# Side work spread anew, priority for the score links, and GELU read from PSUM, in a hybrid transformer block

## The chip, the cores and the metric

The kernel runs on one core of a Trainium2 chip. The metric is the device time of one execution in microseconds (us). Engines are named as the profile names them: PE is the matrix engine, DVE the vector engine, ACT the scalar engine, POOL the general-purpose engine, SP the engine that issues the transfers. Each engine works through its own instructions in their written order; semaphores tie the engines together.

## The reference

One block over 512 tokens of width 2048: adaptive RMS norm, a combined projection, a recurrent group beside a forgetting-attention group, an output projection, and a gated MLP.

```python
mod = c_act @ w_ada[l] + b_ada[l]
sh1, sc1, gt1, sh2, sc2, gt2 = jnp.split(mod, 6, axis=-1)
h = modulate(rms_norm(x, g_mix[l]), sh1, sc1)
proj = h @ w_in[l]
xr, yr, q, k, v, f_logit = jnp.split(proj, splits, axis=-1)
y_rec = rglru_group(xr, yr, ...)          # conv, gates, scan; h * gelu(yr)
y_att = forgetting_attention_group(q, k, v, f_logit, ...)
    # s = q k^T + cum_i - cum_j, causal, softmax, times v; cum = cumsum(log_sigmoid(f))
mix = concat([rms_norm(y_rec, g_out_rec), rms_norm(y_att, g_out_att)])
x = x + gt1 * (mix @ w_out[l])
h2 = modulate(rms_norm(x, g_ffn[l]), sh2, sc2)
gate, up = split(h2 @ w_up[l], 2)
x = x + gt2 * ((silu(gate) * up) @ w_down[l])
```

There are 8 heads of width 128, 8 recurrent blocks of 128 channels, and 5632 hidden channels in the MLP.

## The kernel before

Every product of fp32 operands is made of three fp32r matmuls: both operands are split into a high and a low part (ACT writes the high part, L199 or L192; DVE subtracts it, L200 or L193), and PE adds hi·hi, hi·lo and lo·hi in PSUM (L204). The big products run as stages one after the other, each with its own weights streamed in pages of four contraction tiles (k-tiles):

- w1 (recurrent input), yr0 and yr1 (the gate branch), h0 to h7 (q, k, v of one head each: 16 k-tiles of 12 matmuls, 128 tokens by 384 columns), wo0 to wo3 (output projection), up0, up1 and uf4 to uf43 (MLP in), dn (MLP out).

Small work is hung between the k-tiles of a stage as hooks. In stage h(i+1) the hooks carry the attention of head i. `attention` makes the list: statistics of q and k (`stats`: squares on ACT, reduction L480 on DVE, reciprocal root on POOL L253, product L483 on DVE); transposes to PSUM `qkt` (L490) and their copy out on ACT; four `score` blocks; four `pt_` blocks (transpose of the probabilities, L524) and `pv`. A score block is a short chain over three engines: PE writes s (L510), DVE subtracts it from bt with a running minimum (L514, shown as CUSTOM_DVE_ANT_0 in the trace and ISA in the order), ACT takes the exponential (L516), DVE the reciprocal and the scaling (L517, L518). The decay bt comes from cum: the log-forget values lf are made on DVE in some 18 short steps (L300 to L308, then L434), summed on PE (pc, L436), transposed, written to DRAM as cum_d and read back broadcast as cb.

Other hooks are side work of DVE, each with a load of its own:

- The bias of the three first projections, `bias_in`: 48 loads of 256 KB (bw) and as many products (L592, L594) into three accumulators ba. They hang on h1 and h2, three in a row at every second k-tile; two buffers hold the loads. `bias_sum` (L600, tile binp, in h3) adds them up on PE.
- The adaptive scales, `ada1`: products L149 over loads of 512 KB; five in each of h3 to h6 and so on (`H_ADA`), with lowered priority (`ADA_LATE`).

The order on each engine is chosen by a list scheduler that goes by the written order of the hooks and the priorities; `tc.high_priority(offset=...)` moves work ahead, and what it assumes of times need not be what the chip shows. So an instruction may stand in front of another that is ready sooner.

PSUM has eight banks: four "acc", three "misc" and one "rg". Stage yr1 writes the acc banks and is followed by wo0, also on acc; from there on stages alternate between acc and the other four (`bank`). Between yr1 and wo0, the GELU of four of the recurrent tiles is made from yr1's banks: ACT squares the bank, DVE copies it to SBUF (L766), and two DVE steps L767 and L769 with a tanh between them use the copy. Then the sum of squares of the recurrent outputs (L292) is formed, added on PE (`ratioa`), turned to a ratio on POOL (L250, L253, L269), spread by PE (`ratiob`) and copied by ACT; DVE scales the recurrent tiles (L786), which are split (mx0h by ACT, mx0l and so on by DVE) as the last eight k-tiles of wo0's activation. The attention's outputs are the first eight.

Of the kernel before, what the change touches and what calls it, by code (L numbers as in the profile page):

```python
# [62 lines left out]
def block_kernel(ctx, tc, xT, crow, adaT, vecs, bfr, w1, wyr, wqkv0, wqkv, wgate, wout, wup0, wups, wdown, outT):  # L63
# [408 lines left out]
    def attention(h, q, k, v):  # L472
        st = {}

        def stats():
# [29 lines left out]
        def score(b):  # L505
# [8 lines left out]
            nc.vector.tensor_tensor_reduce(out=p[:, :n], in0=ps[:, :n], in1=p[:, :n], scale=-1.0, scalar=3.0e38,  # L514
                                           op0=ALU.add, op1=ALU.min, accum_out=nm)
            nc.scalar.activation(p[:, :n], p[:, :n], AF.Exp, scale=-1.0, bias=nm, accum_out=sm)  # L516
            nc.vector.reciprocal(sm, sm)  # L517
            nc.vector.tensor_scalar_mul(p[:, :n], p[:, :n], sm)  # L518
# [58 lines left out]
    def bias_load(n):  # L577
        kt, j = divmod(n, 3)
        if kt < KT:
            sd = (w1[kt][:, :512], w1[kt][:, 512:], wyr[0][kt // 4][:, (kt % 4) * 512:(kt % 4 + 1) * 512])[j]  # L580
            bias_src[n] = ap_.tile([P, S], F32, tag="x", name=f"bw{kt}_{j}", bufs=2)
            nc.sync.dma_start(out=bias_src[n], in_=sd)

    def bias_in(kt):
        if kt == 0:
            ba.extend(page(f"ba{j}", "c") for j in range(3))
            bias_load(0)
            bias_load(1)
        for j in range(3):
            src, s1 = bias_src.pop(3 * kt + j), sh1[kt]  # L590
            if kt == 0:
                nc.vector.tensor_scalar_mul(ba[j], src, s1)  # L592
            else:
                nc.vector.scalar_tensor_tensor(out=ba[j], in0=src, scalar=s1, in1=ba[j], op0=ALU.mult, op1=ALU.add)  # L594
            bias_load(3 * kt + j + 2)
# [521 lines left out]
```

## Time and profile before

| | us |
|---|---|
| median of 3 runs | 2153.72 (2149.09 to 2156.75) |
| the profiled execution | 2151.9 |
| its span, first to last instruction | 2150.2 |
| PE busy in the span | 2097.6 (98%) |
| DVE busy in the span | 1533.2 (71%) |

Stages by their times in the trace: w1 0 to 97, yr0 to 150, h0 to 186, h1 to 231, h2 to 279, h3 to 332, h4 to 381, h5 to 430, h6 to 476, h7 to 523, yr1 to 574.6, wo0 to 629.4, wo1 to wo3 to 760, up0 and up1 to 849, uf to 1666, dn to the end. A matmul group in the timeline is one row with its count; the number in brackets is the idle time of the engine just before it, with what ended it. [...]

### The profile page before, as it was taken

How to read it: one execution, taken by the hardware profiler on the slowest of the kernel's cores; microseconds unless marked ns; L12 is line 12 of the kernel's file. 1: busy time of each engine (PE TensorE's matmuls, PEld its weight loads, DVE VectorE, ACT ScalarE, POOL GpSimd, SP SyncE). 2: the span in 40 equal slices, each digit the busy share in tenths (PEclk: the TensorE clock that was granted, in tenths of full speed). 3: DMA queues.
4: the chain of work that ended last, by engine and by line, in shares of the span. 5: the costliest groups of instructions: out<-in, count | busy, mean ns of one | idle time of the engine just before them, and what ended most of it. 6: DMA issues, size and time to landing. Idle time of an engine off the chain costs nothing.

```text
span 2150.2 us, 32261 instructions
## 1 busy us (share of the span) xinstructions
PE 2097.6 (98%) x12737; PEld 1903.2 (89%) x12737; DVE 1533.2 (71%) x2407; ACT 858.1 (40%) x1200; POOL 31.3 (1%) x37
## 2 busy tenths in 40 slices
PE   8999899999999999999999999999999999999998
PEld 6888788888878887999999999999999888888887
DVE  8998668887886689988888888888887443323332
ACT  4433337675432245444444444444444222221111
POOL 0000000000010000000000000000000000000000
PEclk9999999999999999999999999999999999999999
DMA  9987666666777732443444443444445975653442
GB/s 334 349 294 267 190 234 202 222 233 227 258 239 250 251 135 98 146 130 128 136 130 128 136 130 128 136 130 128 136 130 184 334 282 172 213 195 135 155 152 97
DMA packets 133017, 406.01 MB, mean 189 GB/s; under 512 B 14561, under 2 KB 19841, under 8 KB 123138
## 3 DMA queue, kind: packets, MB, share of 16 engines
q1 hardware_dynamic: 132866, 403.96, 55.4%
q8 instruction: 99, 1.62, 0.3%
q14 instruction: 52, 0.43, 0.1%
HBM read 361.15 MB, written 42.75 MB: 188 GB/s over the span
## 4 chain that ended last, share of the span: by engine, by line
PE 82%; DVE 9%; DMA 5%; issue 1%; ACT 1%; POOL 1%; SPq 0%; DVEq 0%; ACTq 0%
PE dn_0p L204 6%; PE dn_3p L204 6%; PE dn_1p L204 6%; PE dn_2p L204 6%; PE w1p L204 4%; PE wo0p L204 2%; PE yr1p L204 2%; PE up0p L204 2%; PE wo3p L204 2%; PE wo2p L204 2%; PE wo1p L204 2%; PE yr0p L204 2%; DMA ada<-in_adaT 2%; DMA bw<-in_w 1%; PE h0p L204 1%
## 5 line engine op out<-in xcount | busy, mean ns | idle before, releaser
L149 DVE SCALAR_TENSOR_TENSOR ada<-ada,c_b 128x1024 f32<-128x1024 f32 x128 | 154.8, 1221 | 49.3 <-DMA ada<-in_adaT 48.9
L200 DVE TENSOR_TENSOR uq_0tl<-uq_0r,uq_0th 128x1024 fp32r<-128x1024 f32 x40 | 49.0, 1225 | 61.7 <-ACT uq_0th L199 61.7
L199 ACT ACTIVATE uq_0sh<-uq_0r 128x1024 fp32r<-128x1024 f32 x40 | 42.5, 1062 | 90.8 <-PE uf10p L989 2.3
L200 DVE TENSOR_TENSOR uq_0al<-uq_0r,uq_0ah 128x1024 fp32r<-128x1024 f32 x40 | 49.0, 1225 | 39.1 <-ACT uq_0ah L199 39.1
L199 ACT ACTIVATE uq_1sh<-uq_1rb 128x1024 fp32r<-128x1024 f32 x40 | 42.5, 1062 | 70.6 <-PE uf43p L989 2.4
L199 ACT ACTIVATE uq_0th<-uq_0r 128x1024 fp32r<-128x1024 f32 x40 | 42.4, 1060 | 70.6 <-DVE uq_0r L969 1.9
L199 ACT ACTIVATE uq_1th<-uq_1ra 128x1024 fp32r<-128x1024 f32 x40 | 42.4, 1061 | 69.7 <-PE uf37p L989 1.8
L199 ACT ACTIVATE uq_1ah<-uq_1ra 128x1024 fp32r<-128x1024 f32 x40 | 42.5, 1061 | 60.6 <-issue 59.1
L199 ACT ACTIVATE uq_0ah<-uq_0r 128x1024 fp32r<-128x1024 f32 x40 | 42.4, 1060 | 49.4 <-issue 46.8
L200 DVE TENSOR_TENSOR uq_1tl<-uq_1ra,uq_1th 128x1024 fp32r<-128x1024 f32 x40 | 49.0, 1225 | 10.3 <-ACT uq_1th L199 10.2
L204 PE MATMUL w1p<-hph,w1h 128*128 128x512 f32 x128 | 47.5, 399 | 6.2 <-ACT hph L345 6.2
L594 DVE SCALAR_TENSOR_TENSOR ba<-bw,sh,ba 128x512 f32<-128x512 f32 x45 | 33.4, 749 | 26.0 <-DMA bw<-in_w 14.9
L200 DVE TENSOR_TENSOR uq_1sl<-uq_1rb,uq_1sh 128x1024 fp32r<-128x1024 f32 x40 | 49.0, 1225 | 3.7 <-ACT uq_1sh L199 1.5
L200 DVE TENSOR_TENSOR uq_0sl<-uq_0r,uq_0sh 128x1024 fp32r<-128x1024 f32 x40 | 49.0, 1226 | 3.6
L204 PE MATMUL w1p<-hpl,w1h 128*128 128x512 f32 x128 | 50.9, 398 | 0.0
L204 PE MATMUL w1p<-hph,w1l 128*128 128x512 f32 x128 | 50.7, 396 | 0.0
L200 DVE TENSOR_TENSOR uq_1al<-uq_1ra,uq_1ah 128x1024 fp32r<-128x1024 f32 x40 | 48.7, 1216 | 0.1
L200 DVE TENSOR_TENSOR dn_1l<-dn_2r,dn_1h 128x1024 fp32r<-128x1024 f32 x11 | 13.5, 1226 | 38.1 <-ACT dn_1h L199 38.1
L159 DVE SCALAR_TENSOR_TENSOR ada<-ada,c_b 128x1024 f32<-128x1024 f32 x32 | 39.0, 1218 | 2.3 <-DMA ada<-in_adaT 2.3
L200 DVE TENSOR_TENSOR dn_0l<-dn_2r,dn_0h 128x1024 fp32r<-128x1024 f32 x11 | 13.5, 1225 | 37.6 <-ACT dn_0h L199 37.6
L200 DVE TENSOR_TENSOR dn_1l<-dn_0r,dn_1h 128x1024 fp32r<-128x1024 f32 x11 | 13.5, 1226 | 37.5 <-ACT dn_1h L199 37.3
L200 DVE TENSOR_TENSOR dn_0l<-dn_0r,dn_0h 128x1024 fp32r<-128x1024 f32 x11 | 13.5, 1226 | 36.9 <-ACT dn_0h L199 36.9
(13787 smaller groups left out, 8165.8 us busy)
## 6 DMA issues: line engine op xcount, KB each, us to landing
ada<-in_adaT SPq DMA_DIRECT2D x160, 512.0 KB, 5.5
uq_0r<-in_wups SPq DMA_DIRECT2D x80, 512.0 KB, 4.1
uq_1ra<-in_wups SPq DMA_DIRECT2D x40, 512.0 KB, 4.0
uq_1rb<-in_wups SPq DMA_DIRECT2D x40, 512.0 KB, 3.3
adf<-in_adaT SPq DMA_DIRECT2D x32, 512.0 KB, 6.0
actd<-ach SPq DMA_DIRECT2D x44, 256.0 KB, 2.1
actd<-acl SPq DMA_DIRECT2D x44, 256.0 KB, 4.1
dn_0r<-in_wdown SPq DMA_DIRECT2D x11, 1024.0 KB, 5.1
```

What stands on the lines that cost most here:

```text
L149: nc.vector.scalar_tensor_tensor(out=t, in0=t, scalar=1.0, in1=cs, op0=ALU.mult, op1=ALU.mult, accum_out=ac)
L159: nc.vector.scalar_tensor_tensor(out=t, in0=t, scalar=1.0, in1=c_b[:, cs], op0=ALU.mult, op1=ALU.mult, accum_out=ada_acc[j][:, hf, i:i + 1])
L199: nc.scalar.activation(R(hi[:, :n]), raw_ap, AF.Copy)
L200: tail_lo.append(nc.vector.tensor_sub(R(lo[:, :n]), raw_ap, hi[:, :n]).ins)
L204: nc.tensor.matmul(ps, lhsT=R(l), rhs=R(r), start=start, stop=stop)
L594: nc.vector.scalar_tensor_tensor(out=ba[j], in0=src, scalar=s1, in1=ba[j], op0=ALU.mult, op1=ALU.add)
```

## The change

1. `bias_in` handles one product at a time, one at each hook `n * 2 // 3` of h1 and h2, with the loads six ahead in pages of tag "c" rather than two buffers. The lowered priority of the adaptive products is dropped, and their hooks move a little.
2. In attention, the norm (L483) becomes a step of its own, three k-tiles (in the last head one) behind the start. The copy of the transposes out of PSUM, the score's DVE and ACT links, and the copy of the transposed probabilities get the priority offset `EVAC` (2500).
3. The GELU's copy to SBUF is gone: L767 and L769 read the PSUM bank. wo0 writes misc and rg, and all later stages use the other set than before; the sums for the three norm factors use acc banks.

```diff
-H_ADA = (3, 4, 7, 10, 14)
+H_ADA = (1, 4, 7, 10, 13)
-ADA_LATE = -300
+BIAS_AHEAD = 6
...
-        with tc.high_priority(offset=ADA_LATE), tc.issue_after(tail_lo[-1]):
+        with tc.issue_after(tail_lo[-1]):
...
             rms_rstd(ss, ss, HEAD_DIM)
+            st["ss"] = ss
+
+        def norm():
+            ss = st["ss"]
             for a, z in ((0, q), (1, k)):
...
-                nc.scalar.activation(zt, pt, AF.Copy, scale=g)
+                with tc.high_priority(offset=EVAC):
+                    nc.scalar.activation(zt, pt, AF.Copy, scale=g)
...
+            with tc.high_priority(offset=EVAC):
+                nc.vector.tensor_tensor_reduce(out=p[:, :n], in0=ps[:, :n], in1=p[:, :n], scale=-1.0, scalar=3.0e38,
+                                               op0=ALU.add, op1=ALU.min, accum_out=nm)
+                nc.scalar.activation(p[:, :n], p[:, :n], AF.Exp, scale=-1.0, bias=nm, accum_out=sm)
+                nc.vector.reciprocal(sm, sm)
+                nc.vector.tensor_scalar_mul(p[:, :n], p[:, :n], sm)
...
-            nc.scalar.activation(pT[:, qs], pt[:, qs], AF.Copy)
+            with tc.high_priority(offset=EVAC):
+                nc.scalar.activation(pT[:, qs], pt[:, qs], AF.Copy)
...
-            bias_src[n] = ap_.tile([P, S], F32, tag="x", name=f"bw{kt}_{j}", bufs=2)
+            bias_src[n] = page(f"bw{kt}_{j}", "c")
...
+    def bias_in(n):
+        if n == 0:
+            ba.extend(page(f"ba{j}", "c") for j in range(3))
+            for m in range(BIAS_AHEAD):
+                bias_load(m)
+        kt, j = divmod(n, 3)
+        src, s1 = bias_src.pop(n), sh1[kt]
         if kt == 0:
...
+        bias_load(n + BIAS_AHEAD)
...
-    ATT_STEPS = (None, 6, 8, 8, 9, 9, 12, 12, 13, 13, 14, 14, 15, 15)
-    LAST_STEPS = (None, 3, 5, 5, 6, 6, 9, 9, 10, 10, 13, 13, 13, 13)
+    ATT_STEPS = (None, 3, 6, 8, 8, 9, 9, 12, 12, 13, 13, 14, 14, 15, 15)
+    LAST_STEPS = (None, 1, 3, 5, 5, 6, 6, 9, 9, 10, 10, 13, 13, 13, 13)
...
-            for kt in range(8):
-                add(hk, kt * 2, lambda kt=kt + 8 * h: bias_in(kt))
+            for n in range(24):
+                add(hk, n * 2 // 3, lambda n=n + 24 * h: bias_in(n))
...
-        g, w = page(f"gy{f}", "c"), page(f"ge{4 + f}", "c")
+        g, w = yr1[f], page(f"ge{4 + f}", "c")
         nc.scalar.activation(w, yr1[f], AF.Square)
-        nc.vector.tensor_copy(out=g, in_=yr1[f])
...
-    rec_sums, rec_spread = rstd_parts(ssq_rec, D_REC, "ratio", times=att_rms)
+    rec_sums, rec_spread = rstd_parts(ssq_rec, D_REC, "ratio", times=att_rms, bank=acc)
...
-        ps = fm_group(wout[g], korder, mix, f"wo{g}", hooks=hk, ps=[bank(g, f, f"wo{g}p{f}") for f in range(4)])
+        ps = fm_group(wout[g], korder, mix, f"wo{g}", hooks=hk, ps=[bank(g + 1, f, f"wo{g}p{f}") for f in range(4)])
...
-        pb = acc(f"bup_p{gi}") if gi % 2 else misc(f"bup_p{gi}")
+        pb = misc(f"bup_p{gi}") if gi % 2 else acc(f"bup_p{gi}")
...
-        ps = [bank(f, b, f"uf{f}p{b}") for b in range(4)]
+        ps = [bank(f + 1, b, f"uf{f}p{b}") for b in range(4)]
...
-            ps = [bank(g + pi, f, f"dn{pi}_{g}p{f}") for f in range(4)]
+            ps = [bank(g + 1, f, f"dn{pi}_{g}p{f}") for f in range(4)]
```

The order of the instructions moves at many places. Three of them follow; a tile's trailing number only tells copies of a tile apart. DVE in stage h1, before, at the end of the log-forget steps (lf; ba<-bw are bias products, h_1l a weight split):

```order
L307 TENSOR_SCALAR lf<-lf 128x32
L616 TENSOR_TENSOR xrl_2739<-xrl_2739,rstd_x 128x512
L200 TENSOR_TENSOR h_1l<-h1r_1999,h_1h 128x768
L306 TENSOR_TENSOR lf<-lf,lfq 128x32
L307 TENSOR_SCALAR lf<-lf 128x32
L594 SCALAR_TENSOR_TENSOR ba_1796<-bw_2_1913,sh_2_1108,ba_1796 128x512
L308 TENSOR_TENSOR lf<-lf,lfs 128x32
L594 SCALAR_TENSOR_TENSOR ba_1794<-bw_0_1916,sh_3_1139,ba_1794 128x512
L434 SCALAR_TENSOR_TENSOR lf<-z,lf 128x32
L438 COPY tot<-pc 128x64
L440 COPY cum<-tot 128x8
```

The same place on DVE after the change (the bias product's line is now L601):

```order
L306 TENSOR_TENSOR lf<-lf,lfq 128x32
L200 TENSOR_TENSOR h_0l<-h1r_2119,h_0h 128x768
L307 TENSOR_SCALAR lf<-lf 128x32
L601 SCALAR_TENSOR_TENSOR ba_1793<-bw_1_2047,sh_6_1248,ba_1793 128x512
L306 TENSOR_TENSOR lf<-lf,lfq 128x32
L601 SCALAR_TENSOR_TENSOR ba_1794<-bw_2_2080,sh_6_1248,ba_1794 128x512
L307 TENSOR_SCALAR lf<-lf 128x32
L601 SCALAR_TENSOR_TENSOR ba_1792<-bw_0_2099,sh_7_1289,ba_1792 128x512
L308 TENSOR_TENSOR lf<-lf,lfs 128x32
L601 SCALAR_TENSOR_TENSOR ba_1793<-bw_1_2102,sh_7_1289,ba_1793 128x512
L434 SCALAR_TENSOR_TENSOR lf<-z,lf 128x32
L601 SCALAR_TENSOR_TENSOR ba_1794<-bw_2_2117,sh_7_1289,ba_1794 128x512
```

A bias product stands now between nearly every two steps of lf. Before the change 10 bias products stood ahead of L434 on DVE, and now there are 23, with the same loads on SP ahead of cum_d's.

DVE in stage h2, before, at the first scores of head 1 (bt<-s):

```order
L200 TENSOR_TENSOR h_1l<-h2r_2420,h_1h 128x768
L594 SCALAR_TENSOR_TENSOR ba_1795<-bw_1_2269,sh_9_1361,ba_1795 128x512
L594 SCALAR_TENSOR_TENSOR ba_1796<-bw_2_2300,sh_9_1361,ba_1796 128x512
L200 TENSOR_TENSOR h_0l<-h2r_2532,h_0h 128x768
L594 SCALAR_TENSOR_TENSOR ba_1794<-bw_0_2303,sh_10_1434,ba_1794 128x512
L594 SCALAR_TENSOR_TENSOR ba_1795<-bw_1_2306,sh_10_1434,ba_1795 128x512
L514 ISA bt_0_2391,nm_0_2441<-s_0_2438,bt_0_2391 128x128
L514 ISA nm_0_2441 128x1
L514 ISA bt_1_2393,nm_1_2450<-s_1_2447,bt_1_2393 128x256
```

The same place on DVE after (L520 is the score's link):

```order
L601 SCALAR_TENSOR_TENSOR ba_1794<-bw_2_2538,sh_15_1643,ba_1794 128x512
L200 TENSOR_TENSOR h_0l<-h2r_2428,h_0h 128x768
L623 TENSOR_TENSOR xrl_2679<-xrl_2679,rstd_x 128x512
L200 TENSOR_TENSOR h_1l<-h2r_2428,h_1h 128x768
L623 TENSOR_TENSOR xrl_2749<-xrl_2749,rstd_x 128x512
L200 TENSOR_TENSOR h_0l<-h2r_2540,h_0h 128x768
L520 ISA bt_0_2399,nm_0_2449<-s_0_2446,bt_0_2399 128x128
L520 ISA nm_0_2449 128x1
L520 ISA bt_1_2401,nm_1_2458<-s_1_2455,bt_1_2401 128x256
L520 ISA nm_1_2458 128x1
```

The bias products that stood ahead of the scores are gone; the last one of all 48 is the first row here. Two products by rstd_x, of the recurrent group's inputs, stand between the weight splits in their place.

PE in stage wo0, before, around the recurrent group's ratio (wo0p are the stage's matmuls; mx15 is the last attention tile, mx0 the first recurrent one):

```order
L265 MATMUL ratioa<-ones,ssq_rec 128x1 x4
L204 MATMUL wo0p_5330<-mx15h,wo_1h 128x512
L204 MATMUL wo0p_5330<-mx15l,wo_1h 128x512
L204 MATMUL wo0p_5330<-mx15h,wo_1l 128x512
L204 MATMUL wo0p_5331<-mx15h,wo_1h 128x512
L204 MATMUL wo0p_5331<-mx15l,wo_1h 128x512
L274 MATMUL rstd_attb<-ident,rstd_attt 128x128 x4
L204 MATMUL wo0p_5331<-mx15h,wo_1l 128x512
L204 MATMUL wo0p_5332<-mx15h,wo_1h 128x512
L204 MATMUL wo0p_5332<-mx15l,wo_1h 128x512
L204 MATMUL wo0p_5332<-mx15h,wo_1l 128x512
L274 MATMUL ratiob<-ident,ratiot 128x128 x4
```

The same steps on PE after:

```order
L204 MATMUL wo0p_5322<-mx14l,wo_1h 128x512
L204 MATMUL wo0p_5322<-mx14h,wo_1l 128x512
L265 MATMUL ratioa<-ones,ssq_rec 128x1 x4
L274 MATMUL rstd_attb<-ident,rstd_attt 128x128 x4
L204 MATMUL wo0p_5323<-mx14h,wo_1h 128x512
L204 MATMUL wo0p_5323<-mx14l,wo_1h 128x512
L274 MATMUL ratiob<-ident,ratiot 128x128 x4
L204 MATMUL wo0p_5323<-mx14h,wo_1l 128x512
L204 MATMUL wo0p_5324<-mx14h,wo_1h 128x512
L204 MATMUL wo0p_5324<-mx14l,wo_1h 128x512
```

`ratioa` moves nine matmuls up, and `ratiob` sixteen, from the end of the attention's eight k-tiles into the seventh of them, two matmuls behind `ratioa` rather than nine.

## Rows read from the trace of the kernel before

**Rows 1.** Page, part 1: busy time, share of the span, instructions of PE.

```profile
PE 2097.6 (98%) x12737; PEld 1903.2 (89%) x12737; DVE 1533.2 (71%) x2407; ACT 858.1 (40%) x1200; POOL 31.3 (1%) x37
```

**Rows 2.** Windows: busy us (instructions) by engine, granted clock, DMA share, GB/s.

```profile
183.00:205.40 22.40, 18.89 (x109) 18.24 (x109) 17.29 (x44) 7.38 (x17) 1.84 (x2) 1.00 0.75 248
231.00:279.00 48.00, 42.37 (x228) 39.32 (x227) 28.58 (x51) 16.77 (x35) 1.84 (x2) 0.93 0.59 186
279.00:332.00 53.00, 48.84 (x262) 46.06 (x261) 37.49 (x71) 21.60 (x43) 1.83 (x2) 0.90 0.68 234
476.00:523.00 47.00, 44.68 (x246) 40.73 (x245) 34.54 (x62) 29.95 (x54) 2.73 (x2) 1.00 0.67 239
574.60:629.40 54.80, 50.30 (x218) 41.05 (x218) 46.55 (x70) 22.23 (x34) 5.64 (x7) 0.94 0.65 221
```

**Rows 3.** Timeline of PE: start, us, instruction, [idle before it <- releaser].

```profile
205.66 0.41 PE L436 MATMUL pc<-lf,triu 128*128 128x32 f32 x2 [3.71 <-DVE lf L434]
...
217.78 0.70 PE L510 MATMUL s<-qkT,qkT 128*128 128x512 f32 x1 [1.28 <-DVE nm L514]
...
262.83 1.22 PE L510 MATMUL s<-qkT,qkT 128*128 128x512 f32 x1 [5.61 <-DVE nm L514]
...
299.62 0.59 PE L600 MATMUL binp<-ones,ba 128*128 128x1 f32 x2 [3.61 <-DVE ba L594]
...
362.93 1.20 PE L510 MATMUL s<-qkT,qkT 128*128 128x512 f32 x1 [2.22 <-DVE nm L514]
...
412.65 0.70 PE L510 MATMUL s<-qkT,qkT 128*128 128x512 f32 x1 [2.57 <-DVE nm L514]
...
513.68 0.66 PE L524 MATMUL pt<-ident,bt 128*128 128x128 f32 x4 [2.32 <-DVE bt L518]
...
592.31 0.39 PE L204 MATMUL wo0p<-mx14h,wo_1h 128*128 128x512 f32 x1
...
598.30 1.13 PE L274 MATMUL ratiob<-ident,ratiot 128*128 128x128 f32 x8
...
601.98 0.80 PE L204 MATMUL wo0p<-mx0h,wo_0h 128*128 128x512 f32 x1 [2.56 <-ACT mx0h L192]
...
612.11 0.78 PE L204 MATMUL wo0p<-mx2l,wo_1h 128*128 128x512 f32 x1 [1.94 <-DVE mx2l L193]
```

**Rows 4.** Timeline of DVE, stage h2, the scores of head 1.

```profile
257.14 0.95 DVE L200 TENSOR_TENSOR h_0l<-h2r,h_0h 128x768 fp32r<-128x768 f32 x1
260.64 0.75 DVE L594 SCALAR_TENSOR_TENSOR ba<-bw,sh,ba 128x512 f32<-128x512 f32 x1 [2.55 <-DMA bw<-in_w]
...
262.48 0.28 DVE L514 CUSTOM_DVE_ANT_0 bt<-s,bt 128x128 f32<-128x128 f32 x1
```

**Rows 5.** Lines of DVE, 186 to 279 us: busy, mean ns | idle before, releaser.

```profile
L594 DVE SCALAR_TENSOR_TENSOR ba<-bw,sh,ba 128x512 f32<-128x512 f32 x36 | 26.7, 749 | 22.8 <-DMA bw<-in_w 12.5 <-DMA bw<-in_wyr 10.4
```

**Rows 6.** Timeline of DVE, stage h1: log-forget chain and first score.

```profile
205.42 0.18 DVE L434 SCALAR_TENSOR_TENSOR lf<-z,lf 128x32 f32<-128x32 f32 x1
...
217.42 0.29 DVE L514 CUSTOM_DVE_ANT_0 bt<-s,bt 128x128 f32<-128x128 f32 x1 [1.21 <-ACT bt L502]
```

**Rows 7.** DMA issues, 150 to 330 us: KB each, median us to landing.

```profile
bw<-in_w SPq DMA_DIRECT2D x30, 256.0 KB, 4.2
```

**Rows 8.** Timeline of DVE, stage h7, an adaptive-scale product.

```profile
508.54 1.23 DVE L149 SCALAR_TENSOR_TENSOR ada<-ada,c_b 128x1024 f32<-128x1024 f32 x1 [3.11 <-DMA ada<-in_adaT]
```

**Rows 9.** Lines of DVE, 573 to 630 us (busy, mean ns).

```profile
L767 DVE SCALAR_TENSOR_TENSOR ge<-ge,gy 128x512 f32<-128x512 f32 x4 | 2.7, 684 | 0.0
L836 DVE TENSOR_TENSOR x<-wo0p,rstd_att 128x512 f32<-128x512 f32 x4 | 2.7, 692 | 0.0
L766 DVE COPY gy<-yr1p 128x512 f32<-128x512 f32 x4 | 2.6, 684 | 0.0
```

**Rows 10.** Timeline of POOL, stage wo0: the ratio.

```profile
595.64 1.10 POOL L250 TENSOR_SCALAR ratiot<-ratiot 128x4 f32<-128x4 f32 x1 [0.27 <-DVE ratiot L266]
...
597.90 0.20 POOL L269 TENSOR_TENSOR ratiot<-ratiot,att_rms 128x4 f32<-128x4 f32 x1
```

More of the change, by code (lines that the diff above doesn't have):

```diff
@@ L513, in score @@
             nm, sm = small(1, f"nm{h}_{b}"), small(1, f"sm{h}_{b}")
[L514 to L518, printed above, removed]
+            with tc.high_priority(offset=EVAC):
[4 more added lines that the diff above has]
+                nc.vector.tensor_scalar_mul(p[:, :n], p[:, :n], sm)
         def pt_(kb):
@@ L549, in attention @@
         L = lambda f, *a: (lambda: f(*a))
-        return [L(stats), L(qk_t), L(score, 0), L(score, 1), L(score, 2), L(score, 3),
+        return [L(stats), L(norm), L(qk_t), L(score, 0), L(score, 1), L(score, 2), L(score, 3),
                 L(pt_, 0), L(pt_, 1), L(pv, 0), L(pt_, 2), L(pv, 1), L(pt_, 3), L(pv, 2), L(pv, 3)]
@@ L580, in bias_load @@
             sd = (w1[kt][:, :512], w1[kt][:, 512:], wyr[0][kt // 4][:, (kt % 4) * 512:(kt % 4 + 1) * 512])[j]
-            bias_src[n] = ap_.tile([P, S], F32, tag="x", name=f"bw{kt}_{j}", bufs=2)
+            bias_src[n] = page(f"bw{kt}_{j}", "c")
             nc.sync.dma_start(out=bias_src[n], in_=sd)
-    def bias_in(kt):
-        if kt == 0:
[L586 to L595, printed above, removed]
+    def bias_in(n):
[5 more added lines that the diff above has]
+        src, s1 = bias_src.pop(n), sh1[kt]
+        if kt == 0:
+            nc.vector.tensor_scalar_mul(ba[j], src, s1)
+        else:
+            nc.vector.scalar_tensor_tensor(out=ba[j], in0=src, scalar=s1, in1=ba[j], op0=ALU.mult, op1=ALU.add)
+        bias_load(n + BIAS_AHEAD)
     def bias_sum():
@@ L773, in block_kernel @@
     st_att = []
-    att_sums, att_spread = rstd_parts(ssq_att, D - D_REC, "rstd_att", inv=att_rms)
-    rec_sums, rec_spread = rstd_parts(ssq_rec, D_REC, "ratio", times=att_rms)
+    att_sums, att_spread = rstd_parts(ssq_att, D - D_REC, "rstd_att", inv=att_rms, bank=acc)
+    rec_sums, rec_spread = rstd_parts(ssq_rec, D_REC, "ratio", times=att_rms, bank=acc)
     def mix_sums():
@@ L933, in block_kernel @@
         if gi == 0:
-            r1_sums, r1_spread = rstd_parts(ssq_1, D, "rstd_1")
+            r1_sums, r1_spread = rstd_parts(ssq_1, D, "rstd_1", bank=acc)
             add(hk, R1STEP[0], r1_sums)
@@ L940, in block_kernel @@
         ps = fm_group(wup0[gi], list(range(KT)), hr, f"up{gi}", hooks=hk, raw_hook=lambda q, raw: up_bias(q, raw, bu_acc),
-                      ps=[bank(gi, f, f"up{gi}p{f}") for f in range(4)])
+                      ps=[bank(gi + 1, f, f"up{gi}p{f}") for f in range(4)])
         up_last = up_fin(gi, ps, bu_acc)
```

## The prediction

> **What bounds the kernel now.** I read the page's busy times first. PE is busy for 2097.6 of 2150.2 us [rows 1], so at most 52.6 us can come from PE waiting less, and a little more from a clock that does not fall. Where those microseconds lie is in the windows by stage: h2 has PE busy for 42.37 of 48.00 us at a granted clock of 0.93, h3 48.84 of 53.00 at 0.90, wo0 50.30 of 54.80 at 0.94, while h7 runs at 1.00 with 2.3 us idle [rows 2]. Last I read the waits one by one in PE's timeline [rows 3]. They have three kinds: PE waits for DVE's link in a score (L514, L518), for the bias accumulators (binp), or for the recurrent group's tiles in wo0 (mx0h, mx2l). In each, DVE or ACT is not short of time over the stage (in h2 DVE is busy for 28.58 of 48.00 us [rows 2]); it stood at something else, in its order, when PE needed it. So the change is worth what it does to that order, and nothing in w1, up, uf or dn, where no such wait stands.
>
> A wait here costs more than its length. PE idled for 5.61 us before 262.83, and the stage has 0.93: 7% of 48.00 us is 3.4 us of clock time below the higher level. After the wait for binp (3.61) the stage has 0.90, which is 5.3 us. After the waits in wo0 (2.56 and 1.94) it has 0.94, 3.3 us. A wait of 2.32 in h7 left 1.00 [rows 2, 3]. Part of the low time lies in the wait itself, where it costs nothing, so I count it at about half to two thirds.
>
> **The change part by part.** All of it is set against the profiled execution: 2150.2 us span and 1.7 around it, 2151.9. That is 1.8 below the median of the runs, 2153.72, well within their spread.
>
> *The bias leaves h2 and h3.* In h2, DVE finishes a weight split at 257.14 + 0.95, then waits 2.55 for a bias load and does two bias products before the first score link at 262.48 [rows 4]; PE's third score waits for that link [rows 3]. Over h1 and h2 the 36 products cost 26.7 us and 22.8 of waiting for loads [rows 5], because two buffers are refilled only when one is free, and a load takes 4.2 us [rows 7]. In the new order nothing of this stands between the split and the link. The link can follow at 258.1, 4.4 earlier; since DVE also lost other waits before, I count 5.2 of the 5.61 and 2.3 of clock: -7.5 (ends -4.4 and -9.0). In h3 PE's wait for binp goes whole, since the last of the 48 products now stands 6 DVE rows ahead of h2's scores: -3.6, and of the 5.3 clock I take a third, 1.7, as the clock stayed low for longer there than after the other waits and may have a second cause: -5.3 (ends -3.6 and -8.9). What is late next in h2 and h3 is a split or the norm's way over POOL, which both stages already have beside their matmuls.
>
> *The bias fills h1.* The same 48 products now stand in h1 and the first half of h2. Ahead of lf's last step L434 there are 23 instead of 10. By DVE's pace (0.67 us from one product's start to the next, the 0.749 of rows 5 less the overlap) the 13 more cost 8.7; the waits for loads that stood there before go. L434 was at 205.42 [rows 6]. In the stretch 183.00 to 205.40 DVE was busy for only 17.29 of 22.40 us [rows 2], so 5.1 us of room takes part of it: L434 at 205.4 + 8.7 - 5.1 = 209.0, up to 211. The loads allow it: 13 more of 0.262 MB beside 248 GB/s at a share of 0.75 make 9.0 MB in place of 5.6, and at a full share (330 GB/s) that takes 27 us, 183 to 210. PE now asks for pc some 30 matmuls and two scores later, 6.3 after 201.95, where it began to wait [rows 3]: 208.2. (From 592.31 to 598.30, eighteen matmuls of 512 columns and two small groups of about 0.9 took 5.99 [rows 3], so 0.238 each, and one of 384 columns three quarters of it, 0.18; thirty make 5.4, the scores 0.9.) So the wait is 1 to 3 in place of 3.71. Behind it cum_d and cb queue on SP after about a dozen more bias loads. The first link came 12.0 after L434 [rows 6]; with those loads, and the transposition placed later on PE, I take 14 to 16, 224 to 226. The last score, which waited 1.28 [rows 3], is now placed at about 222, so 2 to 3, and the transposes behind it wait another 1. In sum 4 to 7 of waits and 1.7 of clock against 3.71 + 1.28 and about 2 of clock: I take +2 (ends -1, and +9 if both loads and links come late).
>
> *Priority for the links.* In h4 the waits are 2.22, in h5 2.57, in h7 2.32 [rows 3]. In the new order the first link of h4 stands two recurrent products earlier, about 1.2 us, and in h5 one link stands ahead of a split of 0.95 behind which it stood. These stages hold up to five adaptive products of 1.23, and one of them waited 3.11 for its load ahead of the softmax of head 7 [rows 8]; that product still stands ahead, but its load is issued before two other transfers. I take -1.5, -1.7 and -1.5 (ends for the three: +1 and -7.1). The norm's own step costs nothing: it still follows the POOL result, which it waited for before, beside the stage's matmuls.
>
> *GELU from PSUM.* Four copies of 0.684 go, 2.7 us of DVE [rows 9]. An operation on 512 columns costs DVE 692 ns with a PSUM operand (L836) and 684 from SBUF (L767) [rows 9], so the eight steps that now read the bank cost about 0.1 more. For the next rows I use 2.4 to 2.6. [...]
>
> *wo0.* The four copies, and a split that now follows the last sum instead of preceding it, put the last L292 about 2.4 to 3 us earlier. `ratioa` is asked for nine matmuls earlier, at 592.31, and `ratiob` two matmuls behind it and rstd_attb, at 594.4. POOL needs 2.5 us between the sums' copy and its last product (595.64 to 597.90 + 0.20) [rows 10], so `ratiob` can start at 595.9: PE waits 1.5 there, which is new. PE's order is fixed, so all matmuls wait behind it. From `ratiob` (598.30) to the first mx0h matmul (601.98) were 3.7 [rows 3]: 599.6 now, while PE with that group (0.9) and the sixteen matmuls that now follow (0.238 each, as above) comes to it at 600.6. So the wait of 2.56 goes, and the place is reached 1.4 earlier. For mx2l, one adaptive product and less stands ahead, and by the same counting DVE has it at about 606.8, and PE asks 6.5 after 600.6; the 1.94 mostly goes. That gives -1.4 - 1.9, and 1.2 of the 3.3 of clock, as the new wait of 1.5 may lower it again: -4.5 (ends 0 and -7).
>
> *Banks.* uf4's first matmul takes the bank of up1's bias sum, so it waits for that copy: I put 0.3, about what POOL waited for a copy of that size, 0.27 [rows 10] (ends 0.2 and 0.8); the other flips only change places. Up and the start of uf are set by DVE's and ACT's splits, which the change leaves.
>
> Sum: -7.5 - 5.3 + 2 - 1.5 - 1.7 - 1.5 - 4.5 + 0.3 = -19.7, 2151.9 - 19.7 = 2132.2. I say 2132; for this case alone the bounds of its terms, which will not all fall on one side, give 2124 to 2139.
>
> **Rivals.** *The waits come back later.* DVE is busy for 34.54 of 47.00 us in h7 and 46.55 of 54.80 in wo0 [rows 2]; the adaptive products no longer stand back, and a load that is late holds all that is queued behind it, as in rows 8. Then h4 to h7 and wo0 gain nothing: -7.5 - 5.3 + 2 + 0.3 = -10.5, 2141. Against it: the links have gone ahead of split work in the order, and the four copies are gone whatever the loads do.
>
> *The loads pace h1.* If the bias loads go at the pace of h1's loads before, 256 KB at 248 GB/s take 1.06 us each, and one product can follow only every 1.06 plus what the weights take: I put 0.63 of waiting on each of the 23, what the 36 had (22.8 / 36) [rows 5]. L434 comes 14.5 later, PE waits for it, and the two clock dips of such a wait add about 2. In place of +2 stands +17: 2147. For it: those loads are wanted in half the time. Against it: they had only two buffers, now six pages.
>
> *Slower.* The same place, further: if each of the 23 waits longer than about (19.7 + 2) / 23 = 0.95 us, h1 loses what all else gains. The price at two loads' time, 2.1 per product, is 1.5 x 23 = 34 us on L434, of which the gains take 22: 2164. The mechanism is bandwidth in h1, whose share was already 0.75 before the 13 more loads [rows 2], with cum_d and cb behind them on the same queue. [...]
>
> *The change does not do what it says.* It speaks of an even spread, and the order shows the opposite: the bias is packed into h1 and the first half of h2. This is in the sum already, and is where it can fail; it has no chance of its own.
>
> **How the numbers follow.** 0.53 for the forecast, 0.04 for better than 2124, 0.20 for the waits that come back, 0.16 for loads that pace h1, 0.07 for slower. Within 0.3% of the median, 2147.3 to 2160.2, a measurement can't be told from no change. Faster is 0.53 + 0.04 + 0.20 and a third of the paced case, 0.82; same is the rest of that and a little of the slower case, 0.12; slower 0.06. The range that leaves out 2 in 10 is 2121 to 2148.
>
> **What would show it.** Right: no wait of PE over 1.5 us in h2's scores and none for binp; granted clocks of 0.97 or more in h2 and h3; pc's wait below 3.7 with L434 near 210; `ratiob` with a new wait of 1 to 2 and no wait for mx0h; rows L767 and L769 at 685 to 700 ns. Wrong: bias products in h1 with a DMA wait each, a wait for pc of 8 or more, or waits for links in h4 to h7 as long as before.

## The result, and the profile after

The changed kernel takes 2129.56 us (median of 4 runs, 2125.76 to 2131.90) against 2153.55 (4 runs) in the same set: a ratio of 0.9888, interval 0.9865 to 0.9911. The prediction was 2132 (2121 to 2148). In a second set it took 2127.43 against 2151.24, 0.9885 (0.9866 to 0.9905).

The page, and the windows by stage (us; busy time and instructions of PE, PEld, DVE, ACT, POOL; granted clock of PE as a share of its full speed, DMA share, GB/s), answer to [rows 1, 2]:

```profile
PE 2090.5 (98%) x12737; PEld 1898.3 (89%) x12737; DVE 1527.9 (72%) x2403; ACT 858.5 (40%) x1200; POOL 33.9 (2%) x37
```

```profile
183.00:209.80 26.80, 25.05 (x145) 24.35 (x145) 24.11 (x56) 8.18 (x18) 2.27 (x2) 1.00 0.88 300
230.30:273.90 43.60, 43.60 (x248) 40.34 (x247) 26.56 (x52) 20.44 (x46) 2.27 (x2) 1.00 0.67 224
273.90:318.30 44.40, 44.40 (x257) 42.65 (x256) 31.45 (x60) 20.80 (x42) 3.33 (x2) 0.96 0.66 218
459.40:502.90 43.50, 43.50 (x239) 39.84 (x239) 33.57 (x62) 29.19 (x51) 2.74 (x2) 1.00 0.77 261
553.70:604.00 50.30, 48.02 (x225) 39.30 (x225) 43.81 (x66) 22.73 (x33) 5.77 (x7) 1.00 0.73 238
827.90:877.80 49.90, 45.86 (x337) 44.91 (x338) 45.50 (x68) 23.78 (x32) 0.00 (x0) 0.90 0.42 137
```

PE is busy 7.1 us less with the same instructions, and its clock was lower for less of the time (on average 0.996 of full speed over the span, 0.992 before); the span is 23.0 shorter. In h2 (second row) PE is busy for all of 43.60 us at a clock of 1.00; before it was 42.37 of 48.00 at 0.93. h3 has no wait left either, yet its clock is 0.96. It fell to 0.50 right behind the matmuls of the bias sum, 24 of one column each, in which PE counts as busy throughout:

```profile
278.15 2.73 PE L607 MATMUL binp<-ones,ba 128*128 128x1 f32 x24
```

```profile
281.20:284.60 3.40, 3.40 (x12) 3.40 (x11) 2.71 (x5) 2.68 (x4) 0.66 (x1) 0.50 0.83 261
```

In nine of ten traces that have the bias out of h2 and h3 the longest of h3's matmuls on the pages h_1 took 522 to 667 ns, as these do at 0.50 (522 here; the median is 334 to 337), and no h3 matmul waits; in the tenth, an experiment told below, the longest took 423 ns and h3 is 42.8 us long. So the low clock of h3 before probably had a second cause beside the wait, as the prediction held possible.

h1, up to lf (first row), moves 300 GB/s at a share of 0.88, against 248 at 0.75. The last row is a stretch that got worse: uf4 with uf5, 49.90 us at a clock of 0.90, where it was 46.70 at 0.96.

The waits of PE that answer to [rows 3] (start, us, instruction, [idle before it <- releaser]):

```profile
210.08 0.41 PE L436 MATMUL pc<-lf,triu 128*128 128x32 f32 x2 [1.71 <-DVE lf L434]
...
226.09 1.62 PE L515 MATMUL s<-qkT,qkT 128*128 128x512 f32 x2 [2.88 <-DVE nm L520]
...
393.62 0.70 PE L515 MATMUL s<-qkT,qkT 128*128 128x512 f32 x1 [1.74 <-DVE nm L520]
...
412.34 0.49 PE L542 MATMUL po<-pT,v 128*128 128x128 f32 x2 [1.87 <-ACT pT L534]
...
576.25 0.60 PE L274 MATMUL ratiob<-ident,ratiot 128*128 128x128 f32 x3 [1.46 <-POOL ratiot L269]
...
590.08 0.50 PE L204 MATMUL wo0p<-mx3h,wo_1h 128*128 128x512 f32 x1 [0.83 <-ACT mx3h L192]
```

The waits for binp, for mx0h and for mx2l are gone, and so is the 5.61 in h2; of h4's 2.22 for a score 0.33 is left, and h7's 2.32 is gone. pc's is 1.71 for 3.71. The last score of head 0 waits 2.88 for 1.28. ratiob's 1.46 is new; so are one of 1.87 for the copy of the last probabilities at the end of h5, and 0.83 for mx3h.

Stage by stage, the starts of the stages' first matmuls give these lengths (us). The columns right of "after" are experiments told below: part 1 alone, part 1 without the adaptive products' edits, part 2 alone, part 3 alone.

| stage | before | after | part 1 | bias only | part 2 | part 3 |
|---|---|---|---|---|---|---|
| h1 | 47.9 | 44.6 | 44.1 | 44.0 | 48.2 | 47.5 |
| h2 | 48.6 | 43.6 | 44.0 | 44.0 | 44.3 | 47.7 |
| h3 | 51.9 | 44.4 | 44.4 | 44.4 | 55.2 | 51.5 |
| h4 | 47.7 | 44.5 | 45.3 | 48.0 | 45.6 | 48.0 |
| h5 | 49.2 | 50.0 | 50.3 | 49.3 | 48.3 | 50.1 |
| h6 | 46.1 | 46.6 | 45.5 | 46.6 | 46.0 | 47.2 |
| h7 | 46.1 | 43.6 | 43.6 | 48.2 | 46.4 | 44.8 |
| yr1 + wo0 | 106.4 | 101.1 | 104.2 | 107.0 | 107.9 | 103.2 |
| uf4 + uf5 | 46.7 | 49.9 | 45.8 | 45.8 | 45.7 | 48.8 |

A stage at 0.96, as h3 after, has lost 4% of 44.4 us to the clock, 1.8; so a single difference under 2 in this table says little.

### The profile page after: what moved, and what is told of

The parts are those of the page before. It is cut to its first block, busy times and chain, and to the rows that moved or that the text cites. A ratio compares the mean times of both kernels' runs of the same rounds, so it can differ in the third digit from the quotient of the medians.

```text
span 2127.2 us, 32243 instructions
## 1 busy us (share of the span) xinstructions
PE 2090.5 (98%) x12737; PEld 1898.3 (89%) x12737; DVE 1527.9 (72%) x2403; ACT 858.5 (40%) x1200; POOL 33.9 (2%) x37
## 4 chain that ended last, share of the span: by engine, by line
PE 88%; DVE 7%; DMA 3%; issue 1%; POOL 1%; ACT 1%; SPq 0%; DVEq 0%; ACTq 0%
PE dn_0p L204 6%; PE dn_3p L204 6%; PE dn_2p L204 6%; PE dn_1p L204 6%; PE w1p L204 4%; PE yr1p L204 2%; PE up0p L204 2%; PE wo3p L204 2%; PE wo2p L204 2%; PE wo1p L204 2%; PE up1p L204 2%; PE yr0p L204 2%; PE wo0p L204 2%; PE h3p L204 2%; PE h2p L204 2%; PE h7p L204 2%
## 5 line engine op out<-in xcount | busy, mean ns | idle before, releaser
L149 DVE SCALAR_TENSOR_TENSOR ada<-ada,c_b 128x1024 f32<-128x1024 f32 x128 | 154.6, 1222 | 47.2 <-DMA ada<-in_adaT 46.8
L199 ACT ACTIVATE uq_0ah<-uq_0r 128x1024 fp32r<-128x1024 f32 x40 | 42.4, 1061 | 49.1 <-issue 46.7
L200 DVE TENSOR_TENSOR dn_0l<-dn_3r,dn_0h 128x1024 fp32r<-128x1024 f32 x10 | 12.3, 1225 | 38.0 <-ACT dn_0h L199 38.0
L159 DVE SCALAR_TENSOR_TENSOR adf<-adf,c_b 128x1024 f32<-128x1024 f32 x32 | 39.1, 1222 | 0.1
```

The source lines that it names most:

```text
L149: nc.vector.scalar_tensor_tensor(out=t, in0=t, scalar=1.0, in1=cs, op0=ALU.mult, op1=ALU.mult, accum_out=ac)
L159: nc.vector.scalar_tensor_tensor(out=t, in0=t, scalar=1.0, in1=c_b[:, cs], op0=ALU.mult, op1=ALU.mult, accum_out=ada_acc[j][:, hf, i:i + 1])
L199: nc.scalar.activation(R(hi[:, :n]), raw_ap, AF.Copy)
L200: tail_lo.append(nc.vector.tensor_sub(R(lo[:, :n]), raw_ap, hi[:, :n]).ins)
```

## The experiments

### Each part of the change alone, and the copies put back

Part 1 is the bias and the adaptive products, part 2 the norm's step and the priorities, part 3 GELU from PSUM and the exchanged banks. Each was put alone on the kernel before. The fourth puts the copies back into the changed kernel and leaves the exchanged banks:

```diff
-        g, w = yr1[f], page(f"ge{4 + f}", "c")
+        g, w = page(f"gy{f}", "c"), page(f"ge{4 + f}", "c")
         nc.scalar.activation(w, yr1[f], AF.Square)
+        nc.vector.tensor_copy(out=g, in_=yr1[f])
```

Part 1 alone:

> The kernel before with the bias and adaptive part of the change alone. Theory (the parts act each in their own stage): h1, h2 and h3 take the lengths of the changed kernel (44.6, 43.6, 44.4 us against 47.9, 48.6, 51.9 before), so -15.8 us, with the waits for h2's score (5.6) and binp (3.6) gone; h4 to h7 stay within 1.5 us of before and wo0 stays at 54.8: about 2136 to 2139. Rival (DVE paces the later stages, so what h2 and h3 gain is given back there): h4 to h7 together 4 us or more longer than before, 2142 or more.

Measured: 2129.48, ratio 0.9892 (0.9871 to 0.9913). Part 1 alone gives all that the whole change gives. h1 to h3 have the lengths expected, but h4 and h7 too are those of the changed kernel, which the theory did not say: -2.4 and -2.5 against before, and no part of links in it. So the time lies below the theory's. h4 to h7 together are 4.5 shorter, not longer, so the rival falls, and with it the prediction's own that the waits come back later.

Part 2 alone:

> The kernel before with the norm as a step of its own and the priority of the links alone. Theory: h2's score still waits, since a bias product with its load stands ahead of the link in this order (wait 3 to 5.6 us), binp's wait of 3.6 stays; h4 gains 2 to 3, h7 2 to 2.6, h5 and h6 nothing: 2146 to 2150. Rival (the priority of the links, not the moved bias, is what frees h2): h2 shorter by 4 us or more, 2143 or less.

Measured: 2146.49, 0.9968 (0.9952 to 0.9984). The time is the theory's, but of the stages that it named only h4 gains (2.1); h7 does not. h2 is 4.3 shorter, as the rival said, and h3 3.3 longer: the link goes ahead of one bias product, while the other still stands in front of it with its load. The last bias product ends only 1.0 us earlier than before, and PE asks for binp 2.2 earlier, so that binp waits longer. DVE and PE in this kernel:

```profile
258.26 0.75 DVE L601 SCALAR_TENSOR_TENSOR ba<-bw,sh,ba 128x512 f32<-128x512 f32 x1 [2.27 <-DMA bw<-in_w]
258.93 0.28 DVE L520 CUSTOM_DVE_ANT_0 bt<-s,bt 128x128 f32<-128x128 f32 x1
```

```profile
259.28 1.55 PE L515 MATMUL s<-qkT,qkT 128*128 128x512 f32 x2 [2.32 <-DVE nm L520]
...
298.60 1.22 PE L607 MATMUL binp<-ones,ba 128*128 128x1 f32 x5 [4.84 <-DVE ba L601]
```

A wait of 2.27 for a load holds the link back to 258.93; PE's wait behind it is 2.32 rather than 5.61, and binp's 4.84 rather than 3.61. Priority shortens the wait here but leaves its cause on the queue.

Part 3 alone:

> The kernel before with GELU from PSUM and the exchanged banks alone. Theory: h1 to h7 as before; wo0 50.3 against 54.8 (-4.5) with a wait of about 1.5 at ratiob in place of the two for mx0h and mx2l; from uf4's first matmul to uf6's 49.9 against 46.7 (+3.2), since with the exchanged banks no matmuls of uf5 are placed into uf4's wait for its split: together -1 to -2, 2151 to 2153. Rival (the +3.2 after up1 is the clock's chance and not the order of PE): 46 to 47.5 there, 2148 to 2150.

Measured: 2148.35, 0.9982 (0.9969 to 0.9996). yr1 and wo0 together are 3.2 shorter, and uf4 with uf5 is 2.1 longer; the theory's signs hold, its +3.2 was 1.1 too large. The time is in the rival's band, but the 48.8 of that stage is not. Against before in the same set the difference is -3.4, with an interval of -0.9 to -6.7, and the theory's -1 to -2 lies in it. h2, h5, h6 and h7 are 0.9 to 1.3 away from before, in both directions, with no edit near them.

The copies put back:

> The changed kernel with the four copies of yr1's banks put back, all else (banks too) as changed. Theory (the copies' 2.7 us of DVE set when the ratio comes): ratioa is asked for nine matmuls later, the sums end 2 to 3 us later, and wo0 is 2 to 3 us longer than the changed kernel's 50.3, 52 to 53.5: 2131 to 2133. Rival (wo0's gain comes from the banks alone, as they free wo0's start and the small sums): wo0 50 to 51, no change from the changed kernel.

Measured: 2133.43, 0.9907 (0.9889 to 0.9925). wo0 is 56.5 against 50.3: more than the theory's 2 to 3. mx0h's wait (1.5) and mx2l's (1.9) come back, and the granted clock of the whole execution is 0.994 against 0.996; what else is in the 6.2 is not shown. The rival falls: the exchanged banks alone save nothing in wo0.

### What inside part 1 does it, and four variants of the changed kernel

Part 1 without its edits of the adaptive products:

```diff
-H_ADA = (1, 4, 7, 10, 13)
+H_ADA = (3, 4, 7, 10, 14)
+ADA_LATE = -300
...
-        with tc.issue_after(tail_lo[-1]):
+        with tc.high_priority(offset=ADA_LATE), tc.issue_after(tail_lo[-1]):
```

> The kernel before with the bias spread and its loads six ahead, and nothing else: the adaptive products keep their hooks and their lowered priority. Theory (h4's and h7's gains in the kernel with bias and adaptive work come from the adaptive products' hooks and priority): h1 to h3 44.2, 44.0, 44.4 as there, but h4 47.7 and h7 46.1 as before, so 5 us more than its 2129.5: 2133 to 2136. Rival (they come from the bias alone, as DVE and the queue enter h4 without a backlog): h4 45 to 46, h7 43.5 to 44.5, 2128 to 2131.

Measured: 2135.14, 0.9919 (0.9897 to 0.9942). The intervals of this ratio and of part 1's overlap, so the stages decide: h4 is 48.0 and h7 48.2, and the theory holds. In all ten traces with the edits of the adaptive products h7 is 43.6, in the four without 44.8 to 48.2. The mechanism is seen on DVE in h7 of this kernel, and of the one with the whole part 1:

```profile
488.33 0.55 DVE L515 CUSTOM_DVE_ANT_0 bt<-s,bt 128x384 f32<-128x384 f32 x1
...
492.85 1.23 DVE L150 SCALAR_TENSOR_TENSOR ada<-ada,c_b 128x1024 f32<-128x1024 f32 x1 [3.96 <-DMA ada<-in_adaT]
...
496.03 1.23 DVE L150 SCALAR_TENSOR_TENSOR ada<-ada,c_b 128x1024 f32<-128x1024 f32 x1 [0.94 <-DMA ada<-in_adaT]
```

```profile
497.91 0.69 PE L525 MATMUL pt<-ident,bt 128*128 128x128 f32 x2 [2.44 <-DVE bt L519]
```

```profile
486.19 1.23 DVE L149 SCALAR_TENSOR_TENSOR ada<-ada,c_b 128x1024 f32<-128x1024 f32 x1 [2.72 <-DMA ada<-in_adaT]
...
489.35 1.22 DVE L149 SCALAR_TENSOR_TENSOR ada<-ada,c_b 128x1024 f32<-128x1024 f32 x1
```

Two adaptive products stand among the links in both. With the edits their loads are issued on SP ahead of two reloads of the recurrent group: DVE waits 2.72 for the first and nothing for the second, where it waited 3.96 and 0.94 as in [rows 8], and PE's wait of 2.44 behind it is gone. The priority of the links is in neither kernel. Which of the two edits does it, the hooks or the dropped low priority, no run separates.

The log-forget steps, cum's transposition and cum_d get the links' priority:

```diff
-            lf = cp.tile([P, NT * NH], F32, name="lf")
+            with tc.high_priority(offset=EVAC):
+                lf = cp.tile([P, NT * NH], F32, name="lf")
...
```

> The changed kernel with the priority of the score links given to the log-forget steps, cum's transposition and cum_d as well; 16 instead of 23 bias products then stand ahead of lf. Theory (bias products between the steps of lf make the waits of 1.7 for pc and 2.9 for the last score that are left in h1): L434 about 4 to 5 us earlier, both waits together under 2.5, h1 42 to 43.5 against 44.6: 2126 to 2128.5. Rival (the read of cb behind the bias loads sets the first link, not lf): first link no earlier than 223, the last score, now asked for 7 us earlier, waits 5 or more, h1 46 or more: 2131 or more.

Measured: 2127.89, 0.9888 (0.9872 to 0.9904): no gain. L434 comes 5.8 earlier and the first link 7.0 earlier (218.68 for 225.73), but PE asks for the last score 7.6 earlier too (215.60 for 223.21):

```profile
204.00 0.18 DVE L435 SCALAR_TENSOR_TENSOR lf<-z,lf 128x32 f32<-128x32 f32 x1
...
218.68 0.29 DVE L522 CUSTOM_DVE_ANT_0 bt<-s,bt 128x128 f32<-128x128 f32 x1 [3.47 <-ACT bt L509]
```

```profile
204.24 0.41 PE L437 MATMUL pc<-lf,triu 128*128 128x32 f32 x2 [1.22 <-DVE lf L435]
...
219.03 0.87 PE L517 MATMUL s<-qkT,qkT 128*128 128x512 f32 x1 [3.43 <-DVE nm L522]
```

pc waits 1.22 and the score 3.43, in sum 4.65 where the changed kernel has 1.71 + 2.88 = 4.59. h1 with h2 is 88.1 against 88.2. Both theory and rival miss: the links come earlier, and the wait moves with them. What is left in h1 is a chain over cum_d and cb, 14.7 from L434 to the link (15.9 in the changed kernel), around which the scheduler places PE's work some 3 us too tightly.

The bias loads two ahead in place of six:

```diff
-BIAS_AHEAD = 6
+BIAS_AHEAD = 2
```

> The changed kernel with the bias loads two ahead in place of six. Theory (six pages are what keeps DVE from waiting for loads in h1, 4.2 us each): DVE's waits for bw in h1 and h2 rise from under 1 us to 10 us or more, but few stand where PE waits; h1 plus h2 88 to 92 against 88.2: 2129 to 2133. Rival (the load's pace was never near): waits stay under 2 us, h1 plus h2 within 0.5: same time.

Measured: 2130.11, 0.9893 (0.9871 to 0.9915), the changed kernel's time. h1 with h2 is 90.7 against 88.2, but not by waits for loads: in h1 the longest matmuls on the pages h_0 took 522 to 631 ns, against 342 to 422. Lines of DVE, 183 to 230 us, of this kernel and of the changed one (busy, mean ns | idle before it, releaser):

```profile
L601 DVE SCALAR_TENSOR_TENSOR ba<-bw,sh,ba 128x512 f32<-128x512 f32 x26 | 18.9, 741 | 0.4 <-DMA bw<-in_wyr 0.4
```

```profile
L601 DVE SCALAR_TENSOR_TENSOR ba<-bw,sh,ba 128x512 f32<-128x512 f32 x35 | 25.6, 744 | 0.4 <-DMA bw<-in_wyr 0.3
```

0.4 us of waits for 26 products, and 0.4 for 35: the theory's 10 us or more did not come. The six in advance are not what freed the loads. The pages fit: with sixteen buffers of the tag a load is issued when the order comes to it, while two buffers, shared with other reloads, held it until a product was done ([rows 5]: 22.8 us of waits for 36). In SP's own waits between 180 and 279 us, the bias loads of the kernel before stood for 21.9 us until a bias product had ended, and those of the changed kernel for 2.5. No run has the even spread on two buffers, so what the spread alone would give is not shown.

The changed kernel on the banks of before (wo0 again on yr1's four), GELU still from PSUM:

```diff
-        ps = fm_group(wout[g], korder, mix, f"wo{g}", hooks=hk, ps=[bank(g + 1, f, f"wo{g}p{f}") for f in range(4)])
+        ps = fm_group(wout[g], korder, mix, f"wo{g}", hooks=hk, ps=[bank(g, f, f"wo{g}p{f}") for f in range(4)])
...
```

The same is done for up, uf, dn and the small sums.

> The changed kernel with the banks of before (wo0 writes yr1's own four banks, while GELU reads them). Theory: PE waits for the last GELU read of a bank at the start of wo0, 4 to 8 us of waits there; wo0 54 to 58 against 50.3; uf4 to uf6 back at 46 to 47 against 49.9: 2129 to 2134. Rival (the banks don't matter for wo0, as GELU is done when they are wanted): wo0 50 to 51, 2124 to 2126.

Measured: 2125.29, 0.9872 (0.9853 to 0.9892). The time is the rival's. The wait at the start of wo0 is there, but only 2.06, not 4 to 8:

```profile
551.52 0.79 PE L204 MATMUL wo0p<-mx8h,wo_0h 128*128 128x512 f32 x1 [2.06 <-DVE ge L775]
```

yr1 and wo0 together are 102.1 against 101.1, and uf4 with uf5 45.8 against 49.9. So the exchange of banks costs there what it saves in wo0, or more. What it costs is in PE's order. In the kernel before (first rows), PE fills uf4's wait for its split with matmuls of uf5; in the changed kernel (last row), with the exchanged banks, the scheduler places none:

```profile
872.47 0.28 PE L989 MATMUL uf4p<-te7h,uq_1cl 128*128 128x256 f32 x1
872.59 0.28 PE L989 MATMUL uf5p<-te0h,uq_0ch 128*128 128x256 f32 x1
...
874.35 0.39 PE L989 MATMUL uf4p<-td4h,uq_1sh 128*128 128x256 f32 x1 [0.40 <-ACT uq_1sh L199]
```

```profile
849.40 0.39 PE L995 MATMUL uf4p<-td4h,uq_1sh 128*128 128x256 f32 x1 [1.60 <-ACT uq_1sh L199]
```

The first ten matmuls of uf5 stand between 872.59 and the wait, which is 0.40; after the change it is 1.60 at the same place, and from 851.20 to 854.40 the clock is 0.50, where it stayed at 1.00 behind the wait before (874.35 to 878.00). All traces agree: the six with exchanged banks have none of these matmuls ahead of the wait, a wait of 1.60, and 47.4 to 50.1 for uf4 with uf5; the eight with the banks of before have ten, a wait of at most 0.40, and 45.7 to 46.7. Why the scheduler doesn't place them stays open: the order shows it, not its reason.

### The last set: which version is best

> The changed kernel once more, as the partner of the next three on one chip: 2127 to 2131, stages within 0.5 us of its first profile except where the clock falls (1.7 us each time).

Measured: 2127.43, 0.9885 (0.9866 to 0.9905), as said above.

> The changed kernel with the banks of before, once more. Theory (the exchanged banks cost 4 us after up1, since no matmul of uf5 fills uf4's wait, and save about 1 at wo0's start): 3 to 5 us below the changed kernel of this set, uf4 to uf6 45 to 46.5 against 48.5 to 50. Rival (the difference of the first run was the clock's chance): within 1.5 us of it.

Measured: 2127.71, 0.9885 (0.9866 to 0.9903): the rival. uf4 with uf5 is 45.8 again, against 48.9, but yr1 and wo0 are 102.9 against 101.3, and h5 is 52.0 against 50.4. The two versions can't be told apart. The profiled executions of the banks of before differ by 7.1 us between the two sets, with the same code: 3.2 of it lies in h5 (48.8 and 52.0) and 1.6 in h3 (42.8 and 44.4).

The copy of the first bank put back, the other three read from PSUM:

```diff
         g, w = yr1[f], page(f"ge{4 + f}", "c")
+        if f == 0:
+            g = page("gy0", "c")
+            nc.vector.tensor_copy(out=g, in_=yr1[f])
```

> The same with the first of the four GELU banks copied to SBUF as before, the other three read from PSUM. Theory (wo0's first matmul waits only for that bank's last read): the wait of 2.1 at wo0's start falls under 0.5 with its slow clock after it, and DVE's 0.7 more is hidden; 1.5 to 3.5 us below the kernel with four PSUM reads, 2122 to 2124. Rival (the wait moves to the second bank, or the ratio comes later by the copy): the same time within 1 us.

Measured: 2128.14, 0.9889 (0.9871 to 0.9908): the rival again. The wait at the start falls to 0.6, and mx2l waits at the end of the ratio's chain:

```profile
590.51 0.80 PE L204 MATMUL wo0p<-mx2l,wo_1h 128*128 128x512 f32 x1 [1.99 <-DVE mx2l L193]
```

The matmuls of wo0 are there earlier, but counted from the start of yr1 `ratiob` comes 1.6 later than with four PSUM reads (75.5 and 73.9). yr1 + wo0 is 105.3.

Part 1 and GELU from PSUM on the banks of before, without part 2:

> The kernel before with the bias and adaptive part and GELU from PSUM on the banks of before, without the norm's own step and the links' priority. Theory (the links' part gives nothing once the bias is out of the way, as h4 45.3 and h7 43.5 were there without it): within 2 us of the kernel with the links, h4 and h5 together 95 to 96. Rival (the links' part is what holds h4 to h7): 4 us or more longer in h4 to h7.

Measured: 2126.18, 0.9881 (0.9861 to 0.9900): part 2 gives nothing that can be measured once part 1 is there; h4 and h5 are 94.4. Against part 1 alone GELU from PSUM gives nothing certain either: yr1 and wo0 are 104.1 and 104.2, and the intervals of the two times overlap. No version beats the changed kernel by more than the measurement tells apart; part 1 alone, with 2129.48, is the simplest that reaches it.

## Why the prediction was right

*The time and its main source.* The sum was -19.7, and the profiled spans differ by 23.0. The largest terms, the bias out of h2 and h3 (-12.8), are measured at -5.0 and -7.5, and part 1 alone is the whole gain. That the sum came so close is in part luck: h2 was put at -7.5 and h3 at -5.3, h1 came 5.3 lower than its term and uf4 with uf5 2.9 higher, and these misses offset each other. In h3 the term of the clock was too small: 1.7 was counted, and by the share of the clock [rows 2] about 5.3 us were lost before and 1.8 after. Two of the signs named in advance miss by a little: h3's clock is 0.96, not 0.97 or more, and the GELU rows are 683 and 684 ns, not 685 to 700. In h2 the link follows the split now, as the order said. DVE after, which answers to [rows 4]:

```profile
252.89 0.96 DVE L200 TENSOR_TENSOR h_0l<-h2r,h_0h 128x768 fp32r<-128x768 f32 x1 [0.68 <-ACT h_0h L199]
253.94 0.29 DVE L520 CUSTOM_DVE_ANT_0 bt<-s,bt 128x128 f32<-128x128 f32 x1
```

*h1.* L434 was put at 209 to 211, the first link at 224 to 226, the last score's wait at 2 to 3, pc's at 1 to 3. DVE after, to [rows 6]:

```profile
209.16 0.76 DVE L601 SCALAR_TENSOR_TENSOR ba<-bw,sh,ba 128x512 f32<-128x512 f32 x1
209.82 0.20 DVE L434 SCALAR_TENSOR_TENSOR lf<-z,lf 128x32 f32<-128x32 f32 x1
...
225.73 0.29 DVE L520 CUSTOM_DVE_ANT_0 bt<-s,bt 128x128 f32<-128x128 f32 x1 [3.23 <-ACT bt L507]
```

All four came as worked out: 209.82, 225.73, 2.88 and 1.71. Yet the term was +2 and h1 became 3.3 shorter. What was mis-sized is the account, not the waits: nine transposes and eight products of head 0, 2.9 us of PE, stood at h1's end before and stand in h2 now. The waits went from 3.71 + 1.28 to 1.71 + 2.88, and h1's clock is 0.96 in both, so h1 itself gained about 0.4 and h2 about 8. h1 and h2 together went from 96.5 to 88.2: -8.3 for the -5.5 of the two terms. The two rivals in which loads pace h1 fall: 35 products wait 0.4 us in all, though a bias load now takes 6.5 us to land and not 4.2. cum_d landed at 218.3 (issued at 215.50, 2.8 us to landing), the last bias load issued ahead of it at 216.2 (211.01 and 5.2). It was little delayed: 2.4 us from issue to landing before and 2.8 after, and 2.2 in the kernel with the log-forget steps first.

*The links.* The step that failed is the one headed "Priority for the links", and in its attribution. It gave -4.7 for h4, h5 and h7; measured -3.2, +0.8 and -2.5, -5.0 in sum, close by size and by luck. But part 1 alone gives -2.4, +1.0 and -2.5, with the old order of links, while part 2 alone gives -2.1, -0.9 and +0.3: h4 gains by either, and the two gains do not add up; h7 gains by part 1 only. In h7 it was the load of the adaptive product, issued earlier; I had that fact and filed it under the wrong edit. In h5 the wait of 2.57 became 1.74, and one of 1.87 at its end took its place.

*GELU and wo0.* The rows of L767 and L769 (L773 and L775 now) answer to [rows 9]; busy, mean ns | idle:

```profile
L775 DVE SCALAR_TENSOR_TENSOR ge<-ge,yr1p 128x512 f32<-128x512 f32 x4 | 2.7, 683 | 0.0
...
L773 DVE SCALAR_TENSOR_TENSOR ge<-ge,yr1p 128x512 f32<-128x512 f32 x4 | 2.6, 684 | 0.0
```

683 and 684 ns with a PSUM operand, 684 and 685 from SBUF before: these rows show no penalty. The 8 ns of L836, which reads wo0's bank, were taken from another kind of operation. So all of the copies' 2.7 us of DVE are saved; the lower end of the 2.4 to 2.6 that the prediction used for the next rows was the author's estimate, and no run shows it. On the exchanged banks wo0 is 56.5 with the copies and 50.3 without. ratiob waits 1.46 where 1.5 was worked out. wo0 was put at -4.5, and is 54.8 to 50.3. That the two agree exactly is luck, as about half of it is not the edit: part 1 alone has 52.5, with nearly the same waits (2.55, 1.68) and a clock of 1.00 instead of 0.94:

```profile
554.10:606.60 52.50, 47.98 (x217) 38.35 (x218) 44.49 (x67) 22.06 (x34) 5.64 (x7) 1.00 0.68 223
```

```profile
581.85 0.50 PE L204 MATMUL wo0p<-mx0h,wo_0h 128*128 128x512 f32 x1 [2.55 <-ACT mx0h L192]
...
591.06 0.50 PE L204 MATMUL wo0p<-mx2l,wo_1h 128*128 128x512 f32 x1 [1.68 <-DVE mx2l L193]
```

These are that stage's window and PE's timeline in part 1 alone.

*Banks.* "so it waits for that copy: I put 0.3" was the mis-sized term: uf4 with uf5 is 3.2 longer. What costs it is not the copy of the bias sum, but the place of uf5's matmuls in PE's order. I had compared wo0's order and not that of uf4.

## What to carry to other kernels

Side work with loads of its own, hung in groups before a short chain that another engine waits for, cost a load's wait there: in h2 DVE waited 2.55 for a bias load ahead of the score link, and PE 5.61 for the link [rows 3, 4]. So give its loads enough buffers and let it run where nothing is waited for, before raising priorities. What a part is worth must be measured without the others: here the three gave -22, -5 and -3 us each alone and -24 together. And a change of PSUM banks can change PE's order far behind it, as here in uf4, where PE waited 1.60 for 0.40 without ten matmuls of uf5, so the order has to be read to the end of the program.
